# A hybrid encoder block in fp32: another order of first loads, zero products in front, and sums of squares moved from VectorE to GpSimd

## The chip, the cores and the metric

The kernel runs on one core of a Trainium2 chip. The metric is device time in microseconds (us) of one execution. TensorE is called PE, its weight loads PEld, VectorE DVE, ScalarE ACT, GpSimd POOL, and SyncE, whose queue issues nearly all loads, SP.

## The reference, cut to what matters

One layer over 512 tokens of width 2048, all in float32:

```
xn = rmsnorm(x, norm_mix)            # mean of squares over the 2048 channels
y  = xn @ W_in                       # 2048 x 7552, split in two groups of heads
h  = x + concat[GDN(y), RWKV7(y)] @ W_out
h += CrossAttn(rmsnorm(h), rmsnorm(mem))
h += square(relu(rmsnorm(h) @ W_up)) @ W_down
out = rmsnorm(h)
```

The change touches only the beginning: `rmsnorm(x)` and the first products of `xn @ W_in`.

## The kernel before, in words

Channels lie on the 128 partitions and tokens along the free dimension, so `x` is 16 tiles of 128x512 (k = 0 to 15). Every float32 operand of the big products is split into a high part in the PE's faster format (fp32r) and the rest: `hi = cast(v)`, `lo = v - hi`. A product is then three matmuls, hi·hi, hi·lo and lo·hi. For `x` the channel gain `norm_mix` is put in at the split (`xin`): ACT writes `xhi`, DVE writes `xlo` by one scalar_tensor_tensor. The token's factor `rstd` of the rmsnorm is the same for all channels, so it is multiplied in when a finished column tile of `y` is taken out of PSUM (`evict`), and the products can start before it is known.

`projections` runs the 59 column tiles of `W_in`. The first two (n = 0, 1) run side by side, six matmuls for each k, so that few x tiles feed many matmuls; from n = 2 on a tile has 16 x 3 matmuls of its own. Weights come in pieces of 128x1024 (eight k): `loader` loads a piece into `wraw` (three buffers), ACT casts it to `whi`, DVE subtracts to `wlo`. The very first two pieces are cut in halves so that PE can start on 512 columns: `pieceload` loads the first half into a tile `sg`, `pieces` splits it, `rawload` brings the other half. The third and fourth piece (second half of k, n = 0 and 1) go to tiles named `wBK` (hi), `wAR` (lo) and `wGA` (hi), `wGB` (lo).

The x tiles lie in sixteen buffers that are free at the start, and the profile calls them by these names: k = 0 `gq`, 1 `gk`, 2 `gv`, 3 `gz`, 4 `gkn`, 5 `gqn`, 6 `gEs`, 7 `gEG`, 8 `gqd`, 9 `gAq`, 10 `gkt`, 11 `tA`, 12 `E` (or `E2`), 13 `k`, 14 `kp`, 15 `Kt`. `xsum` makes the sum of squares: ACT squares a tile into `sr` (two buffers, in turn) and it is added to an accumulator whose name is `r`. One matmul with ones (`pss`) sums over partitions, and ACT makes `rstd` of it by a logarithm and an exponential. All parameters (`prm`, 262 columns) come in one load.

Up to the end of the attention's key products (some 1050 us), the order on every engine is made by a planner inside the program: each chain (`xin`, `xsum`, `pieces`, `loader`, `projections`, a chain for each head, ...) yields its next operation; `run` takes the one whose inputs are ready first by a cost table (`cost`) and its rank, and `issue` puts it on its engine's queue. Its cost table has a fixed price for each kind of operation, and nothing for one engine holding up another. The engines then work through these queues strictly in order, waiting by semaphores. Behind that stage the order is written out by hand.

The lines that decide the part in question:

```
xr[k] = tl(("gq", "gk", "gv", "gz", "gkn", ...)[k])     # load of x tile k
yield from split_(xr[k], hi, lo, col("norm_mix", k))    # xin: ACT, then DVE
sq = short()                                            # xsum: one of two sr buffers
yield AC.activation(sq, xr[k], AF.Square)
yield DV.tensor_tensor(out=acc, in0=acc, in1=sq, op=ALU.add)
```

Of the kernel before, what the change touches and what calls it, by code (L numbers as in the profile page):

```python
# [9 lines left out]
F32 = mybir.dt.float32  # L10
F32R = mybir.dt.float32r
AF = mybir.ActivationFunctionType
ALU = mybir.AluOpType
# [4 lines left out]
P = 128  # L18
# [55 lines left out]
def build(tc, I, out):  # L74
    nc = tc.nc
    V, S, GP, PE = nc.vector, nc.scalar, nc.gpsimd, nc.tensor
# [9 lines left out]
    pq = pq_cm.__enter__()  # L86

    prm = pc.tile([P, NPRM], F32, name="prm")
    nc.sync.dma_start(prm, I["prm"])
    NC0 = 256  # L90
    cst0 = pc.tile([P, NC0], F32, name="cst0")
    cst = pq.tile([P, NCST - NC0], F32, name="cst")
# [5 lines left out]
    def col(name, i=0):  # L98
        o, w = PRM[name]
        return prm[:, o + i:o + i + 1]  # L100
# [17 lines left out]
    def psb(nm, tag="mx", bufs=2):  # L118
        return tile_of(ps, [P, 512], F32, tag, nm, bufs)

    def mm(o, l, r, start=True, stop=True, again=False):
        PE.matmul(o, l, r, start=start, stop=stop, skip_group_check=again)  # L122
# [17 lines left out]
    def wraw():  # L140
        wcnt[0] += 1
        return tile_of(pw, [P, 1024], F32, "wraw", f"wraw{wcnt[0]}", NWR)
# [32 lines left out]
    def tile_of(pool, shape, dt, tag, nm, bufs):  # L175
        t = pool.tile(shape, dt, tag=tag, name=nm, bufs=bufs)
        turns[tag] = turns.get(tag, -1) + 1
        slot[t.tensor.name] = (tag, turns[tag] % bufs)
        holder[tag, turns[tag] % bufs] = t.tensor.name
        return t  # L180
# [6 lines left out]
    def where(a):  # L187
        n = a.tensor.name
        k = slot.get(n, n)
        assert holder.get(k, n) == n, (n, holder[k])  # L190
        return (k, part(a)) if k in parted else k
# [16 lines left out]
    DV, AC, GS, TE, SY = (Lane(e, k) for e, k in ((V, "DVE"), (S, "ACT"), (GP, "POOL"), (PE, "PE"), (nc.sync, "SP")))  # L208

    def cost(op):  # L210
        eng, nm, _, a, k, out, ins, _ = op
        n = out.free_size()
        if eng == "PE":
            l = ins[0]
            if l.dtype == F32R:
                return n * 0.417 + (13.3 if state["shape"] is None else 120.0)
            sh = (l.partition_size(), l.free_size())
            sw = 0 if state["shape"] == sh or sh == (128, 128) else 100
            if nm == "transpose":
                return sw + (110 if sh[0] > 64 else 40)  # L220
            if sh == (64, 64):
                return sw + (32 if op[5].tensor.name[:2] in ("ri", "gi", "pa", "pv", "pu", "pw", "pk", "po", "pp") else 59)
            if sh[0] < 128 and n == 512:
                return sw + 530
            return sw + (115 if sh[0] < 128 and n == 128 else 2 * max(n * 0.84, 114))
        if eng == "DVE":
            if nm == "memset":
                return 60 + 0.3 * n
            if nm == "tensor_scalar":
                return 210 + 0.45 * n  # L230
            if nm == "tensor_tensor_scan":
                return 90 + 2.2 * n
            return 190 + 1.05 * n if nm == "scalar_tensor_tensor" else 154 + 1.05 * n
        if eng == "ACT":
            need = {AF.Tanh: "e", AF.Ln: "l", AF.Exp: "e"}.get(a[2] if len(a) > 2 else None)
            return (140 + 0.885 * n + 80 * sum(isinstance(x, bass.AP) for x in k.values())
                    + (40 if len(a) > 2 else 0) + (1283 if need and need != state["table"] else 0))
        if eng == "POOL":
            return 116 + 0.75 * n if nm == "memset" else 235 + 2.3 * n
        return 100.0  # L240

    def start(op):
        eng, out = op[0], where(op[5])
        t = clock[eng]
        for b, log in [(where(i), landed) for i in op[6]] + [(out, landed), (out, seen)]:
            x, by = log.get(b, (0.0, eng))
            if op[1] == "dma_start" and by == "DMA" and b == out and log is landed:
                continue
            t = max(t, x + op[7][0] + (0.0 if by == eng else CROSS))
        return t  # L250

    def issue(op):
        eng, nm, f, a, k, out, ins, slack = op
        t = start(op)
        d = cost(op)
        f(*a, **k)  # L256
        if nm == "dma_start":
            clock[eng] = t + (60 if eng == "ACT" else 620 if any(x.tensor.name[:2] in ("bg", "nd") for x in [out] + ins) else 330)
            size = math.prod(out.shape) * 4
            state["dma"] = max(state["dma"], t + 330) + size / 300  # L260
            t, eng = max(state["dma"] + 700, t + 2900) + slack[1], "DMA"
        else:
            t += d
            clock[eng] = t
        if eng == "PE":
            state["shape"] = None if ins[0].dtype == F32R else (ins[0].partition_size(), ins[0].free_size())
        if eng == "ACT" and len(a) > 2 and a[2] in (AF.Tanh, AF.Ln, AF.Exp):
            state["table"] = "l" if a[2] == AF.Ln else "e"
        landed[where(out)] = (t, eng)
        for i in ins:  # L270
            b = where(i)
            if seen.get(b, (0.0, 0))[0] < t:
                seen[b] = (t, eng)
# [7 lines left out]
    def after(*ev):  # L281
        return lambda: ev in events
# [45 lines left out]
    def split_(src, hi, lo, gain=None):  # L328
        if gain is None:
            yield AC.copy(hi, src)  # L330
            yield DV.tensor_tensor(out=lo, in0=src, in1=hi.bitcast(F32), op=ALU.subtract)
        else:
            yield AC.activation(hi, src, AF.Copy, scale=gain)
            yield DV.scalar_tensor_tensor(out=lo, in0=src, scalar=gain, in1=hi.bitcast(F32),
                                          op0=ALU.mult, op1=ALU.subtract)
# [20 lines left out]
    rstd = pc.tile([P, T], F32, name="rstd")  # L356
# [6 lines left out]
    def tl(tag, w=512, bufs=1, shape=None):  # L363
        cnt[0] += 1
        return tile_of(pm, shape or [P, w], F32, tag, f"{tag}_{cnt[0]}", bufs)
# [52 lines left out]
    raws, halves, used, whole, piece = {}, {}, set(), set(), {}  # L418

    def pieceload(i):  # L420
        piece[i] = tl("sg", 512, NSH["sg"])
        return SY.dma_start(piece[i], wq[i][1][:, 0:512])

    def rawload(i):
        raws[i] = wraw()
        if i in piece:
            return SY.dma_start(raws[i][:, 512:], wq[i][1][:, 512:])
        o = raws[i] if len(wq[i][1].shape) == 2 else raws[i].rearrange("p (a b) -> p a b", b=M)
        return SY.dma_start(o, wq[i][1])
# [39 lines left out]
    def pieces():  # L469
        for i in piece:  # L470
            halves[i] = hi, lo = wsplit()
            yield from split_(piece[i], hi[:, 0:512], lo[:, 0:512])
            events.add(("piece", i))

    def half(i):
# [3 lines left out]
    xhi, xlo = [], []  # L479
    acc = tl("r")  # L480
    xr = {}
    XA = 8

    def xload(k):
        xr[k] = tl(("gq", "gk", "gv", "gz", "gkn", "gqn", "gEs", "gEG", "gqd", "gAq", "gkt", "tA", "E2", "k", "kp", "Kt")[k])
        return SY.dma_start(xr[k], I["xT"][:, k, :])

    def xin():
        for k in range(KD):
            hi, lo = act_tile(f"xhi{k}"), act_tile(f"xlo{k}")  # L490
            yield from split_(xr[k], hi, lo, col("norm_mix", k))
            xhi.append(hi)
            xlo.append(lo)
            if k + XA < KD:
                yield xload(k + XA)

    def xsum():
        yield AC.activation(rstd[:, 0:1], b_one, AF.Ln)
        for k in range(KD):
            yield lambda: len(xhi) > k  # L500
            if k == 0:
                yield AC.activation(acc, xr[k], AF.Square)
            else:
                sq = short()
                yield AC.activation(sq, xr[k], AF.Square)
                yield DV.tensor_tensor(out=acc, in0=acc, in1=sq, op=ALU.add)
        yield after("consts")
        pt = psb("pss", "scr", 1)
        yield TE.matmul(pt, ones, acc, start=True, stop=True)
        yield from rsq_(rstd, pt, 1.0 / 2048, b_eps6)  # L510
# [742 lines left out]
    def ahead():  # L1253
        yield after("rows")
        for j in range(NSET):
            chain(presums([tl(f"ds{j}{i}", PIECE, shape=[P, PIECE]) for i in range(4)], PIECE, after("kp", 15)),
                  lambda eng: 2 if eng == "SP" else PRANK)

    issue(pieceload(0))
    issue(xload(0))  # L1260
    issue(pieceload(1))
    issue(xload(1))
    issue(rawload(0))
    issue(rawload(1))
    for k in range(2, 6):
        issue(xload(k))
    issue(rawload(2))
    for k in range(6, XA):
# [430 lines left out]
    acc = ph.tile([P, T], F32, tag="acc", name="acc2", bufs=1)  # L1699
    alloc(range(7))  # L1700
    for n in range(KD):
        if n < 2:
            pt = begun[n][0]
            attend(*begun[n], 1)
        else:
            pt = psb(f"at{n}", "mm", 2)
# [712 lines left out]
```

## Time and profile before

| | |
|---|---|
| time before, median of 3 runs | 2906.9 us (2904.82, 2906.92, 2906.9) |
| profiled execution, own time | 2904.46 us |
| its span, first to last instruction | 2902.7 us |
| PE busy | 2870.4 us (99% of the span) |
| DVE, ACT, POOL busy | 2330.4, 1570.0, 223.6 us |
| PE waits for its first operand | 7.8 us |
| granted PE clock, mean | 0.998 |

A row of the timeline gives start, duration, engine, line, operation, output<-inputs and shape; in brackets the idle time of the engine just ahead of it and what ended that. A duration contains start-up and tail that overlap with the next instruction: the distance between the starts of two rows that follow each other is what an instruction costs its engine. L256 is the planner's `issue`, through which most instructions go, so tiles tell them apart. In the program's order, a name may carry the number of its buffer.

### The profile page before, as it was taken

Reading aid. Unit: us, or ns where it says so; the run is one execution under the profiler, and the core shown is the slowest. Engines: PE = TensorE matmul, PEld = TensorE weight load, DVE = VectorE, ACT = ScalarE, POOL = GpSimd, SP = SyncE. Lnnn points to the kernel's source line nnn. Section 1 sums busy time; section 2 is a strip of 40 time slices with the busy share of each in tenths; the row PEclk is TensorE's granted clock in tenths of the full one; section 3 lists DMA queues with packets and bytes.
Section 4 is the critical chain, followed back from the end, with each engine's and each line's share of the span. In section 5 each row is a group of like instructions: output and inputs, shape, how many; then the busy total and the mean of one; then the engine's idle time right before and its main releaser. Section 6 shows DMA issues by size and latency. Waiting matters only on the chain.

```text
span 2902.7 us, 49242 instructions
## 1 busy us (share of the span) xinstructions
PE 2870.4 (99%) x18794; PEld 2420.3 (83%) x18794; DVE 2330.4 (80%) x3547; ACT 1570.0 (54%) x2233; POOL 223.6 (8%) x547
## 2 busy tenths in 40 slices
PE   8999999999999999999999999999999999999998
PEld 7877877787877888889988888888888888888887
DVE  7787787787887877769956898898998878787888
ACT  6454555555655655564445656555555645454544
POOL 0213213213223000000000000000000000000000
PEclk9999999999999999999999999999999999999999
DMA  5646656656666788784423354565566868978733
GB/s 190 175 139 184 164 156 181 160 150 187 176 163 188 219 249 280 227 286 159 127 92 95 106 163 152 193 199 193 186 201 191 283 225 278 295 257 272 270 100 109
DMA packets 319773, 553.02 MB, mean 191 GB/s; under 512 B 100968, under 2 KB 186220, under 8 KB 319536
## 3 DMA queue, kind: packets, MB, share of 16 engines
q1 hardware_dynamic: 292144, 518.41, 58.0%
q10 hardware_dynamic: 27392, 31.46, 3.1%
q8 instruction: 147, 2.41, 0.3%
q14 instruction: 90, 0.74, 0.1%
HBM read 443.45 MB, written 106.31 MB: 189 GB/s over the span
## 4 chain that ended last, share of the span: by engine, by line
PE 93%; DMA 3%; DVE 2%; ACT 1%; issue 1%; POOL 0%; ACTq 0%; SPq 0%; DVEq 0%; POOLq 0%
PE py L256 22%; PE mxu L256 12%; PE mgu L256 6%; PE mgd L256 6%; PE mxd L256 6%; PE op L122 6%; PE vp L122 3%; PE sc L122 3%; PE at L122 3%; PE mmd L256 3%; PE kp L256 3%; PE mmu L256 3%; PE scrd L256 3%; PE scgd L256 3%; PE kq L256 3%; PE vo L122 1%
## 5 line engine op out<-in xcount | busy, mean ns | idle before, releaser
L256 ACT CAST whi<-wraw 128x1024 fp32r<-128x1024 f32 (+1 forms) x366 | 383.7, 1049 | 399.8 <-PE py L256 146.8
L256 DVE TENSOR_TENSOR wlo<-wraw,whi 128x1024 fp32r<-128x1024 f32 (+1 forms) x366 | 450.4, 1231 | 102.7 <-ACT whi L256 92.9
L256 PE MATMUL py<-xhi,whi 128*128 128x512 f32 x928 | 372.2, 401 | 7.8 <-ACT xhi L256 7.8
L256 PE MATMUL py<-xlo,whi 128*128 128x512 f32 x928 | 373.7, 403 | 0.0
L256 PE MATMUL py<-xhi,wlo 128*128 128x512 f32 x928 | 372.9, 402 | 0.0
L256 ACT CAST whi<-w 128x1024 fp32r<-128x1024 f32 x176 | 185.4, 1054 | 203.9 <-PE mxu L256 48.3
L256 DVE TENSOR_TENSOR wlo<-w,whi 128x1024 fp32r<-128x1024 f32 x176 | 214.8, 1221 | 51.5 <-ACT whi L256 49.5
L256 PE MATMUL mxu<-cb,whi 128*128 128x512 f32 x1016 | 255.0, 392 | 0.0
L256 PEld LDWEIGHTS py<-xhi,whi 128*128 128x128 f32 x928 | 175.0, 189 | 42.1 <-ACT xhi L256 7.8
L256 PEld LDWEIGHTS mxu<-cb,whi 128*128 128x128 f32 x1016 | 182.8, 189 | 32.7
L256 PEld LDWEIGHTS py<-xlo,whi 128*128 128x128 f32 x928 | 175.0, 189 | 35.5 <-DVE xlo L256 0.9
L256 PEld LDWEIGHTS py<-xhi,wlo 128*128 128x128 f32 x928 | 175.1, 189 | 35.1 <-issue 1.8
L131 DVE TENSOR_TENSOR wlo<-wraw,whi 128x1024 fp32r<-128x1024 f32 x112 | 136.6, 1221 | 45.5 <-ACT whi L130 42.5
L130 ACT CAST whi<-wraw 128x1024 fp32r<-128x1024 f32 x112 | 117.7, 1051 | 85.5 <-PE op L122 29.1
L256 PEld LDWEIGHTS mxu<-cb,wlo 128*128 128x128 f32 x1016 | 138.7, 190 | 10.5 <-DVE wlo L256 0.7
L256 PE MATMUL mxu<-cb,wlo 128*128 128x256 f32 x1016 | 142.2, 282 | 0.3 <-DVE wlo L256 0.3
L256 ACT ACT_TABLE_LOAD x87 | 111.6, 1283 | 36.4 <-DVE suml_gn L256 15.5
L256 PE MATMUL mgu<-cb,whi 128*128 128x512 f32 x512 | 129.4, 394 | 1.4 <-ACT whi L256 1.3
L256 PE MATMUL mxd<-whi,cb 128*128 128x512 f32 x512 | 126.7, 389 | 0.0
L256 PE MATMUL mgd<-whi,cb 128*128 128x512 f32 x512 | 126.5, 389 | 0.0
L256 ACT CAST whi<-ws 128x1024 fp32r<-128x1024 f32 x75 | 78.9, 1052 | 75.4 <-PE mgu L256 49.2
L122 PE MATMUL op<-ob,whi 128*128 128x256 f32 (+1 forms) x752 | 115.3, 304 | 0.0
(946 smaller groups left out, 6452.3 us busy)
## 6 DMA issues: line engine op xcount, KB each, us to landing
wraw<-in_w_in SPq DMA_DIRECT2D x116, 512.0 KB, 4.5
wraw<-in_w_up SPq DMA_DIRECT2D x65, 512.0 KB, 3.8
w<-in_w_up SPq DMA_DIRECT2D x63, 512.0 KB, 3.9
ds<-in_w_dm SPq DMA_DIRECT2D x128, 205.0 KB, 4.0
sd_s<-ds SPq DMA_DIRECT2D x128, 205.0 KB, 5.2
wraw<-sd_s SPq DMA_DIRECT2D x51, 512.0 KB, 5.1
w<-sd_s SPq DMA_DIRECT2D x50, 512.0 KB, 5.0
w<-in_w_dm SPq DMA_DIRECT2D x48, 512.0 KB, 5.1
```

The lines of the kernel that those rows point to most:

```text
L122: PE.matmul(o, l, r, start=start, stop=stop, skip_group_check=again)
L130: S.copy(hi, src)
L131: V.tensor_tensor(out=lo, in0=src, in1=hi.bitcast(F32), op=ALU.subtract)
L256: f(*a, **k)
```

## The change

1. The first x tile (`gq`) is loaded from ACT's queue, ahead of everything on it; on SP's queue the first weight half comes first.
2. Of the parameters only the 16 columns of `norm_mix` are loaded at the start, into a tile `prm0` that `xin` uses; all 262 columns follow behind the two second weight halves.
3. x tiles 1, 2 and 3 are loaded ahead of the second weight halves.
4. The two first weight halves (`sg`) are cast on DVE, not on ACT, and the second of them only when the first x tile is split.
5. The 15 additions of the sum of squares run on POOL, not on DVE.
6. Fifteen float32 matmuls of a 128x128 block of zeros with itself stand in front on PE (`warm`, outside the planner). They write to a PSUM tile that nobody reads.

```diff
-    nc.sync.dma_start(prm, I["prm"])
+    prm0 = pq.tile([P, 16], F32, name="prm0")
...
     def pieces():
         for i in piece:
             halves[i] = hi, lo = wsplit()
-            yield from split_(piece[i], hi[:, 0:512], lo[:, 0:512])
+            if i:
+                yield lambda: len(xhi) > 0
+            yield DV.tensor_copy(hi[:, 0:512], piece[i])
+            yield DV.tensor_tensor(out=lo[:, 0:512], in0=piece[i], in1=hi[:, 0:512].bitcast(F32), op=ALU.subtract)
             events.add(("piece", i))
...
-    def xload(k):
+    def xload(k, SY=SY):
...
-            yield from split_(xr[k], hi, lo, col("norm_mix", k))
+            yield from split_(xr[k], hi, lo, prm0[:, k:k + 1])
...
-                yield DV.tensor_tensor(out=acc, in0=acc, in1=sq, op=ALU.add)
+                yield GS.tensor_tensor(out=acc, in0=acc, in1=sq, op=ALU.add)
...
+    warm = rstd[:, P:2 * P]
+    V.memset(warm, 0.0)
+    pt = psb("warm", "scr", 1)
+    for _ in range(15):
+        mm(pt[:, 0:P], warm, warm)
+    issue(xload(0, Lane(nc.scalar, "ACT")))
     issue(pieceload(0))
-    issue(xload(0))
+    issue(SY.dma_start(prm0, I["prm"][:, 0:16]))
     issue(pieceload(1))
     issue(xload(1))
+    issue(xload(2))
+    issue(xload(3))
     issue(rawload(0))
     issue(rawload(1))
-    for k in range(2, 6):
+    issue(SY.dma_start(prm, I["prm"]))
+    for k in range(4, 6):
         issue(xload(k))
```

Since the planner's clock now runs otherwise, it also orders other instructions anew. On ACT, the stretch from the cast of the third weight piece (`wBK`) to that of the fourth (`wGA`) stood like this before (`xhi` rows split an x tile, `sr` rows square one):

```order
L256 CAST wBK<-wraw_219 128x1024
L256 ACTIVATE xhi_320<-gEs_221,prm 128x512
L256 ACTIVATE sr_330<-gv_211 128x512
L256 ACTIVATE xhi_347<-gEG_223,prm 128x512
L256 ACTIVATE xhi_358<-gqd_255,prm 128x512
L256 ACTIVATE xhi_369<-gAq_269,prm 128x512
L256 CAST wGA<-wraw_277 128x1024
```

The same stretch of ACT now:

```order
L256 CAST wBK<-wraw_238 128x1024
L256 ACTIVATE xhi_345<-gEs_240,prm_73 128x512
L256 ACTIVATE sr_355<-gkn_234 128x512
L256 ACTIVATE xhi_374<-gEG_242,prm_73 128x512
L256 ACTIVATE xhi_386<-gqd_267,prm_73 128x512
L256 ACTIVATE xhi_397<-gAq_282,prm_73 128x512
L256 ACTIVATE xhi_404<-gkt_292,prm_73 128x512
L256 ACTIVATE xhi_412<-tA_305,prm_73 128x512
L256 ACTIVATE sr_379<-gqn_236 128x512
L256 CAST wGA<-wraw_321 128x1024
```

Three rows more (x tiles 10 and 11 and a square) now stand between `wBK` and `wGA`. On DVE, in the stretch that ends with the low part of the fourth piece (`wGB`), the order was:

```order
L256 SCALAR_TENSOR_TENSOR xlo_311<-gqn_217,prm,xhi_310 128x512
L256 TENSOR_TENSOR r_178<-r_178,sr_279 128x512
L256 TENSOR_TENSOR wAR<-wraw_219,wBK 128x1024
L256 SCALAR_TENSOR_TENSOR xlo_321<-gEs_221,prm,xhi_320 128x512
L256 SCALAR_TENSOR_TENSOR xlo_348<-gEG_223,prm,xhi_347 128x512
L256 SCALAR_TENSOR_TENSOR xlo_359<-gqd_255,prm,xhi_358 128x512
L256 SCALAR_TENSOR_TENSOR xlo_370<-gAq_269,prm,xhi_369 128x512
L256 TENSOR_TENSOR r_178<-r_178,sr_330 128x512
L256 TENSOR_TENSOR wGB<-wraw_277,wGA 128x1024
```

And on DVE now:

```order
L256 TENSOR_TENSOR wAR<-wraw_238,wBK 128x1024
L256 SCALAR_TENSOR_TENSOR xlo_346<-gEs_240,prm_73,xhi_345 128x512
L256 SCALAR_TENSOR_TENSOR xlo_375<-gEG_242,prm_73,xhi_374 128x512
L256 SCALAR_TENSOR_TENSOR xlo_387<-gqd_267,prm_73,xhi_386 128x512
L256 SCALAR_TENSOR_TENSOR xlo_398<-gAq_282,prm_73,xhi_397 128x512
L256 SCALAR_TENSOR_TENSOR xlo_405<-gkt_292,prm_73,xhi_404 128x512
L256 SCALAR_TENSOR_TENSOR xlo_413<-tA_305,prm_73,xhi_412 128x512
L256 TENSOR_TENSOR wGB<-wraw_321,wGA 128x1024
```

The sums (`r_178`, the accumulator) are gone from DVE, and `wGB` stands two x tiles later. On POOL the sums are now in front of and behind three memsets:

```order
L256 TENSOR_TENSOR r_178<-r_178,sr_379 128x512
L256 TENSOR_TENSOR r_178<-r_178,sr_421 128x512
L256 MEMSET WTz 128x896
L256 MEMSET BTz 128x896
L256 MEMSET TtG 128x512
L256 TENSOR_TENSOR r_178<-r_178,sr_442 128x512
L256 TENSOR_TENSOR r_178<-r_178,sr_482 128x512
```

Six sums stand ahead of the memsets (the last two of them are shown) and nine behind. On PE, `pss` stands 16 rows earlier in the sequence of `py` matmuls (129 of them stand ahead of it). From the inversion of the fifth RWKV head (`ri4`) to the end of the planned stage, PE's order is that of before.

## The prediction

> **What bounds the kernel now.** I read the page first, then PE's waits, then the timeline of the first 25 us.
>
> ```profile
> span 2902.7 us, 49242 instructions
> PE 2870.4 (99%) x18794; PEld 2420.3 (83%) x18794; DVE 2330.4 (80%) x3547; ACT 1570.0 (54%) x2233; POOL 223.6 (8%) x547
> PE py L256 <- ACT xhi L256: 7.8, 1, 7.8
> PE kp L256 <- ACT whi L256: 2.4, 1, 2.4
> PE pkk L256 <- DVE gk L256: 2.2, 1, 2.2
> PE ri7u L256 <- DVE k L256: 2.0, 1, 2.0
> ```
>
> PE is busy 99% of the span, so nearly every microsecond by which its stream of matmuls is put off or brought forward at the start is still there at the end. Its longest wait is the first: 7.8 us until the first x tile is split. The next three lie where PE's order is that of before, so I leave them as they are.
>
> The timeline shows what the first 7.8 us are made of (SPq rows are issues of loads):
>
> ```profile
> 0.75 0.40 SPq L89 DMA_DIRECT2D prm<-in_prm  x1
> 1.21 0.42 SPq L256 DMA_DIRECT2D sg<-in_w_in  x1
> 1.67 0.43 SPq L256 DMA_DIRECT2D gq<-in_xT  x1
> 4.92 0.62 ACT L256 CAST whi<-sg 128x512 fp32r<-128x512 f32 x1 [2.68 <-DMA sg<-in_w_in]
> 7.04 0.72 ACT L256 ACTIVATE xhi<-gq,prm 128x512 fp32r<-128x512 f32 x1 [1.50 <-DMA gq<-in_xT]
> 7.82 0.79 PE L256 MATMUL py<-xhi,whi 128*128 128x512 f32 x1 [7.82 <-ACT xhi L256]
> ...
> 11.33 0.60 PE L256 MATMUL py<-xlo,whi 128*128 128x512 f32 x1
> 11.76 0.41 PE L256 MATMUL py<-xhi,wlo 128*128 128x512 f32 x1
> ...
> 15.66 0.39 PE L256 MATMUL py<-xhi,whi 128*128 128x512 f32 x1
> 15.88 0.39 PE L256 MATMUL py<-xlo,whi 128*128 128x512 f32 x1
> ```
>
> Three loads stand in a row (131, 256 and 256 KB); ACT starts at each landing. Matmuls start 0.43 us apart up to 11.76 and 0.22 to 0.23 apart later: PE runs at half its clock for its first 3.9 us. The row at 15.66 is the first matmul on x tile 4 (`gkn`).
>
> **The change part by part: what it gains.** The first matmul needs `gq`, the weight half and `norm_mix`. Before, 387 KB (prm and sg) had landed at 4.92 and 643 KB at 7.04. Now sg, gq and 8 KB of parameters are 520 KB: in proportion 6.0 us. With the ACT split (0.72) and the hand-over that the rows show (7.04 to 7.82) `xhi` reaches PE at 6.8. The zero products must be through by then as well. Float32 products of 128 columns are in the trace, at full clock:
>
> ```profile
> 200.40 0.60 PE L256 MATMUL gpo<-gAq,gE 128*128 128x128 f32 x4
> ...
> 201.88 0.48 PE L256 MATMUL py<-xlo,whi 128*128 128x512 f32 x1
> ```
>
> Between these two rows stand 14 passes of `gpo` (two a product): 0.106 us a pass. Fifteen products are 30 passes, 3.2 us at full and 6.4 us at half clock. They begin behind DVE's memset, about 1.2 us, so they end between 4.4 and 7.6; if the clock rises 3.9 us after their start, as it did after 7.82, it rises at 5.1 and they end at 6.4. The first real product comes at about 7.0 (6.8 to 7.6), and at full clock: its eight slow matmuls up to 11.76 took 3.9 us and would take 8 x 0.23 = 1.8. Casting `sg` on DVE costs between 0.42 (tensor_scalar of 128x512, next row) and 0.69 us (tensor_tensor, below); I take 0.45, and it lies in DVE's wait for the first x tile.
>
> ```profile
> 57.13 0.42 DVE L256 TENSOR_SCALAR gAq<-gAq 128x512 f32<-128x512 f32 x1
> 5.30 0.63 SPq L256 DMA_DIRECT2D gkn<-in_xT  x1
> gkn<-in_xT SPq DMA_DIRECT2D x1, 256.0 KB, 7.5
> ```
>
> So PE may run up to 2.9 us ahead, but loads cap it. Ahead of `gkn` the queue holds the same bytes as before and 8 KB more. It was issued at 5.30 and landed 7.5 us later, at 12.8; split and handed over it reaches PE at 13.6, against 15.66 before. At the fifth tile PE is ahead by 2.1 us at most.
>
> **What it gives back: the order of ACT and DVE.** The fourth weight piece (`wGA`, `wGB`) is needed for the 54th matmul. These rows show that need and the costs on the way:
>
> ```profile
> 22.27 0.39 PE L256 MATMUL py<-xhi,wGB 128*128 128x512 f32 x1
> ...
> 18.34 0.71 ACT L256 ACTIVATE xhi<-gAq,prm 128x512 fp32r<-128x512 f32 x1
> 18.98 1.06 ACT L256 CAST wGA<-wraw 128x1024 fp32r<-128x1024 f32 x1
> 19.94 0.72 ACT L256 ACTIVATE xhi<-gkt,prm 128x512 fp32r<-128x512 f32 x1
> 20.56 0.62 ACT L256 ACTIVATE sr<-gz 128x512 f32<-128x512 f32 x1
> 21.08 0.71 ACT L256 ACTIVATE xhi<-tA,prm 128x512 fp32r<-128x512 f32 x1
> ...
> 16.09 1.23 DVE L256 TENSOR_TENSOR wAR<-wraw,wBK 128x1024 fp32r<-128x1024 f32 x1
> 17.23 0.75 DVE L256 SCALAR_TENSOR_TENSOR xlo<-gEs,prm,xhi 128x512 fp32r<-128x512 f32 x1
> 17.89 0.75 DVE L256 SCALAR_TENSOR_TENSOR xlo<-gEG,prm,xhi 128x512 fp32r<-128x512 f32 x1
> ```
>
> By the distances of starts an x tile costs ACT 0.62, a 1024 cast 0.96, a square or a 512 cast 0.52; DVE pays 1.14 for a 1024 difference and 0.66 for an x tile. On ACT, from the split of `gkn` (12.8) to the cast `wGA`, there now stand eight x tiles (5.0), one 512 cast and three squares (2.1) and `wBK` (1.0): 8.1 us, so `wGA` starts at 20.9 and ends at 21.9. The difference `wGB` (1.2) is then ready at 23.1 if DVE does nothing else. Before, PE had it at 22.27 without waiting. So a lead of 2.1 us turns into a delay of 0.8 here, even without POOL.
>
> **What POOL adds.** Fifteen sums of 0.69 us leave DVE and go to POOL. An add of this size on POOL, and what happens beside it, are in the trace:
>
> ```profile
> L256 DVE TENSOR_TENSOR r<-r,sr x15: 681/692/693, 15.5 to 42.3; 128x512 f32<-128x512 f32 x15
> 119.50 1.29 POOL L256 TENSOR_TENSOR gEs<-gE,cst 128x512 f32<-128x512 f32 x1
> 120.13 1.75 DVE L256 TENSOR_TENSOR wlo<-wraw,whi 128x1024 fp32r<-128x1024 f32 x1 [0.17 <-ACT whi L256]
> ...
> 346.40 1.36 DVE L256 TENSOR_TENSOR wlo<-wraw,whi 128x1024 fp32r<-128x1024 f32 x1 [1.39 <-ACT whi L256]
> 346.97 1.94 POOL L256 TENSOR_TENSOR gEs<-gE,cst 128x512 f32<-128x512 f32 x1 [0.30 <-ACT gE L256]
> ```
>
> POOL needs 1.29 us. The DVE difference that began 0.63 us into it took 1.75 instead of 1.23: it stood until POOL was done. At 346.97 it was the other way round: POOL took 1.94, the excess of 0.65 being what the difference that ended at 347.76 still had to run. So these two exclude each other, less some 0.15 us at the edge. [...]
>
> In the stretch that decides, DVE works through eight x tiles (5.3), a 512 difference (0.6), two small parameter rows (0.2), `wAR` (1.1) and `wGB` (1.2), 8.4 us from 13.6: it would be through at 22.0, inside the 23.1 above. Three of POOL's sums (the squares in ACT's stretch) fall among them, each holding DVE for 1.29 - 0.15 = 1.14 us: 3.4 us more, so `wGB` is ready at 25.4 rather than 23.1. PE waits twice on the way, about 2.5 us for `xlo` of `gEs` (behind `wAR` and a sum) and 2.5 us for `wGB`, and its 54th matmul starts at 25.4 instead of 22.27: **+3.1 us**. With edges of 0.05 or 0.25 us and one sum more or less in the stretch it is +1.7 to +3.8; without any exclusion +0.8.
>
> Next comes `pss`, which PE takes in order; behind it stand the matmuls of n = 2 and 3. It needs all 15 sums. After the 54th matmul 76 stand ahead of it: 25.4 + 76 x 0.23 = 42.9. POOL has ten sums (12.9) and three memsets (0.84 + 0.84 + 0.52 in the trace's rows, 2.1 by starts) from about 23.2: 38.2 bare. Seven DVE instructions come between (four `xlo`, three `wlo`), holding POOL for up to 0.5 or 1.0 us each, 5.0 at most; I take 3. The sums are done at 41 to 43: `pss` just about does not wait. **0**.
>
> **The clock gate.** Does PE lose its full clock in those two waits? Three stretches of 3.41 us, the width of the one in which the trace has a lower clock (busy PE, PEld, DVE, ACT, POOL, then PEclk):
>
> ```profile
> 916.30:919.71 3.41, 2.45 (x43) 1.92 (x42) 0.91 (x3) 1.46 (x4) 0.00 (x0) 1.00 1.00 363
> 929.95:933.37 3.42, 1.44 (x65) 1.20 (x64) 2.92 (x6) 1.75 (x3) 2.15 (x5) 1.00 0.32 92
> 933.37:936.78 3.41, 3.41 (x16) 2.65 (x9) 3.26 (x5) 1.41 (x4) 3.01 (x6) 0.50 0.56 175
> ```
>
> With PE busy 1.44 of 3.42 us (the 2.0 us wait for `ri7u`) the next stretch ran at 0.50; with 2.45 it stayed full. In such a stretch about 8 matmuls pass instead of 15, 1.7 us lost. A wait of 2.5 us leaves too little in one stretch if most of it falls into one, which depends on where the stretches lie: I take one chance in two for the second wait (a loss behind the first is swallowed by the second): **+0.9**. [...]
>
> **The sum.** +3.1 + 0 + 0.9 = +4.0 us, on the profiled execution's 2904.46 (1.8 us more than its span) 2908.5. The median of the runs is 2906.9, 2.4 above the profiled one; on it the forecast is **2910.9**. A measurement of this kernel can tell about 0.2%, 5.8 us, from no change: the forecast lies within that. The rest of PE's order hardly changes its mix, and its waits up to the fifth head are small, for which I allow 1 us either way.
>
> **The rivals.** *Slower than the bound:* the sums end late. If each of the seven DVE instructions holds POOL for its whole length (4 x 0.66 + 3 x 1.14 = 6.1), the sums end at 44.3 and `pss` holds PE 1.4 us; with the clock halved after `wGB`, 3.1 + 1.4 + 1.7 = +6.2, and with +3.8 at `wGB` +6.9: 2913.1 to 2913.8. It decides from the point where the last sum ends after 42.9. For it: exclusion is plain in both pairs of rows. Against: the edges overlap, and a halved clock gives POOL time. 33%.
>
> *The exclusion hardly bites:* sums fall into gaps of DVE, and only ACT's order counts: +0.8, 2907.7. For it: the difference at 346.40 ran before POOL and lost little (0.13). 11%.
>
> *Faster than the bound:* the lead of 2.1 us stays (the fourth piece lands and is cast in time), the halved clock at 933 is not met (1.7), and of the three late waits (6.6 together) about a third goes: -6.0, 2900.9. Against: those waits stand behind an unchanged order, and ACT alone puts `wGA` at 20.9. 6%.
>
> *The zero products do not do what they are for:* they end at 7.6, or the clock falls again in the short waits for the first `xlo`. That costs up to 2.1 us before the fifth tile and nothing behind it, since the wait for `wGB` swallows it; it is inside the forecast.
>
> **How the numbers follow.** Forecast 50%, the two others within the bound or over it as given: same 0.50 + 0.11 = 0.61, slower 0.33, faster 0.06. The range leaves out the faster rival and the far end of the slow one: 2904.5 (hardly any exclusion, 0.8, on the lower of the runs, 2904.82, and 1 us of luck) to 2915.0 (slow rival and 1 us).
>
> **What would show it.** First real matmul near 7.0 and starts 0.23 apart; `xhi` of `gkn` near 12.8; PE's row on `wGB` near 25.4, behind a wait on DVE `wlo` or `xlo` of 2 to 3 us; POOL's sums and DVE's two-input rows stretched in turn; `pss` near 43. Wrong is the forecast if `wGB` is there by 23, or if PE is held at `pss` by more than 2 us.

## The result, and the profile after

The changed kernel takes 2913.2 us (median of 7 runs, 2911.28 to 2917.1), the kernel before in runs on the same chip 2903.5 (7 runs, 2902.16 to 2906.92): a ratio of 1.0032, 95% interval 1.002 to 1.0043. That is 9.7 us more by the medians, over the bound of 0.2%. The predicted time of 2910.9 us lay too low, the range (to 2915.0) holds the median, and the outcome lies on the side of the slow rival.

The profiled execution took 2911.63 us (before 2904.46). Its page and its list of PE's waits (us in total, times, longest):

```profile
span 2909.8 us, 49302 instructions
PE 2878.7 (99%) x18824; PEld 2427.2 (83%) x18824; DVE 2338.9 (80%) x3543; ACT 1569.7 (54%) x2231; POOL 248.5 (9%) x562
PE py L256 <- DVE xlo L256: 2.7, 3, 1.4
PE py L256 <- DVE wGB L256: 2.6, 1, 2.6
PE kp L256 <- ACT whi L256: 1.7, 1, 1.7
PE ri7u L256 <- DVE k L256: 1.4, 1, 1.4
```

The span is 7.1 us longer. The first wait of 7.8 us is gone; 5.3 us for `xlo` and `wGB` stand in its place, and the late waits for `kp` and `ri7u` are 1.3 us shorter than before. The beginning on PE, from its timeline:

```profile
1.18 5.67 PE L122 MATMUL warm<-rstd 128*128 128x128 f32 x30 [1.18 <-DVE rstd L1263]
6.60 0.48 PE L256 MATMUL py<-xhi,whi 128*128 128x512 f32 x1
12.55 0.39 PE L256 MATMUL py<-xhi,whi 128*128 128x512 f32 x1
25.49 0.51 PE L256 MATMUL py<-xhi,wGB 128*128 128x512 f32 x1 [2.59 <-DVE wGB L256]
44.56 1.02 PE L256 MATMUL pss<-r,cst 128*128 128x512 f32 x2
```

At x tile 4 (12.55) PE is 3.1 us ahead of before (15.66); at the 54th matmul (25.49) it is 3.2 behind (22.27). In between, ACT, DVE and POOL:

```profile
11.14 0.72 ACT L256 ACTIVATE xhi<-gkn,prm 128x512 fp32r<-128x512 f32 x1 [0.54 <-DMA gkn<-in_xT]
19.09 1.03 ACT L256 CAST wGA<-wraw 128x1024 fp32r<-128x1024 f32 x1
20.65 0.62 ACT L256 ACTIVATE sr<-gEs 128x512 f32<-128x512 f32 x1
...
14.08 1.79 DVE L256 SCALAR_TENSOR_TENSOR xlo<-gqn,prm,xhi 128x512 fp32r<-128x512 f32 x1
15.79 1.31 DVE L256 TENSOR_SCALAR prm<-prm 128x1 f32<-128x1 f32 x2
19.49 1.78 DVE L256 SCALAR_TENSOR_TENSOR xlo<-gqd,prm,xhi 128x512 fp32r<-128x512 f32 x1
21.86 1.78 DVE L256 SCALAR_TENSOR_TENSOR xlo<-gkt,prm,xhi 128x512 fp32r<-128x512 f32 x1
24.22 1.21 DVE L256 TENSOR_TENSOR wGB<-wraw,wGA 128x1024 fp32r<-128x1024 f32 x1
...
13.66 1.66 POOL L256 TENSOR_TENSOR r<-r,sr 128x512 f32<-128x512 f32 x1 [1.62 <-ACT sr L256]
15.74 1.30 POOL L256 TENSOR_TENSOR r<-r,sr 128x512 f32<-128x512 f32 x1 [0.42 <-ACT sr L256]
19.32 1.40 POOL L256 TENSOR_TENSOR r<-r,sr 128x512 f32<-128x512 f32 x1 [2.28 <-ACT sr L256]
21.41 1.68 POOL L256 TENSOR_TENSOR r<-r,sr 128x512 f32<-128x512 f32 x1 [0.69 <-ACT sr L256]
25.09 15.56 POOL L256 TENSOR_TENSOR r<-r,sr 128x512 f32<-128x512 f32 x9
```

`wGA` is cast by 20.1, but the difference `wGB` only starts at 24.22, because four DVE rows behind 13.6 took about 1.04 us more than they do alone (an `xlo` 0.74; the two parameter rows at 15.79, merged into one line, 0.27 in e9 below): each waited for a sum of POOL's. The parameter rows have a single input of 128x1. POOL's last nine sums took 1.73 us each, in turn with DVE's rows, and were done at 40.65, ahead of `pss` at 44.56. Behind the wait PE's granted clock falls to 0.50 (the columns are those of the prediction's stretches):

```profile
22.59:26.00 3.41, 0.82 (x4) 0.46 (x3) 3.41 (x4) 2.50 (x4) 3.41 (x5) 1.00 0.70 281
26.00:29.41 3.41, 3.41 (x9) 2.65 (x9) 3.41 (x3) 2.19 (x3) 3.25 (x3) 0.50 0.86 207
```

### The profile page after: what moved, and what is told of

Its sections match the earlier page's. It is cut to its first block, busy times and chain, and to the rows that moved or that the text cites. A ratio compares the mean times of both kernels' runs of the same rounds, so it can differ in the third digit from the quotient of the medians.

```text
span 2909.8 us, 49302 instructions
## 1 busy us (share of the span) xinstructions
PE 2878.7 (99%) x18824; PEld 2427.2 (83%) x18824; DVE 2338.9 (80%) x3543; ACT 1569.7 (54%) x2231; POOL 248.5 (9%) x562
## 4 chain that ended last, share of the span: by engine, by line
PE 91%; DMA 3%; DVE 2%; ACT 1%; issue 1%; POOL 0%; ACTq 0%; SPq 0%; DVEq 0%; POOLq 0%
PE py L256 21%; PE mxu L256 12%; PE mgd L256 6%; PE mxd L256 6%; PE mgu L256 6%; PE op L122 5%; PE vp L122 3%; PE sc L122 3%; PE at L122 3%; PE mmd L256 3%; PE mmu L256 3%; PE kp L256 3%; PE scrd L256 3%; PE scgd L256 3%; PE kq L256 3%
```

## The experiments

Times are medians, the ratio is to the kernel before in runs on the same chip; "wGB" is the start of the 54th matmul. Span, wGB and the stretches at half clock (their starts up to 1140 us) are those of the one profiled execution; a number in brackets tells how many stretches follow each other.

| kernel | time, us | ratio, 95% | span | wGB | half clock at |
|---|---|---|---|---|---|
| before | 2903.5 to 2904.7 | 1 | 2902.7 | 22.27 | 933 |
| after | 2913.2 | 1.0032 [1.002, 1.0043] | 2909.8 | 25.49 | 26, 924 |
| e1 memsets for sums | 2907.3 | 1.0011 [1.0002, 1.0019] | 2905.0 | 21.96 | 920 |
| e2 sums on DVE, order of after | 2909.3 | 1.0014 [1.0005, 1.0023] | 2909.6 | 22.99 | 920, 1131 |
| e9 first six sums on DVE | 2908.3 | 1.0018 [1.0009, 1.0026] | 2909.6 | 22.50 | 226, 922, 1134 |
| e10 sums of half width | 2908.2 | 1.0014 [1.0005, 1.0023] | 2907.7 | 22.54 | 922 |
| e3 before, sums on POOL | 2910.7 | 1.0021 [1.0012, 1.003] | 2910.1 | 23.31 | 38 |
| e5 after without part 5 | 2906.4 | 1.0002 [0.9993, 1.001] | 2907.8 | 21.87 | 935 |
| e4 before and zeros | 2905.2 | 1.0001 [0.9992, 1.001] | 2903.0 | | 933 |
| e6 after, one zero product | 2914.3 | 1.0036 [1.0024, 1.0048] | 2912.5 | 25.84 | 26, 924 |
| e7 before, early loads | 2910.5 | 1.0023 [1.0014, 1.0032] | 2904.6 | | 926 |
| e11 before, early loads, zeros | 2903.8 | 1.0001 [0.9992, 1.001] | 2901.3 | | none |
| e8 another plan | 2910.4 | 1.0023 [1.0015, 1.0031] | 2912.9 | | 225, 501, 692, 928 |
| e12 a second other plan | 2930.8 | 1.0095 [1.0081, 1.0109] | 2931.2 | | 593 (2), 835 (3), 849 (2), 859 (2) |

Theory: GpSimd's sums hold DVE, DVE is late with `wGB`, and the wait there halves the clock. Rivals: the new order, the new loads or the zeros cost the time.

**e1, the sums replaced by memsets of POOL** (1.47 us for a sum's 1.30, in the same places of the same order; the sums are left out):

```diff
-yield GS.tensor_tensor(out=acc, in0=acc, in1=sq, op=ALU.add)
+o = GS.tensor_tensor(out=acc, in0=acc, in1=sq, op=ALU.add)
+def fill(out, in0, in1, op):
+    for c in (512, 512, 240):
+        GP.memset(in1[:, 0:c], 0.0)
+yield o[:2] + (fill,) + o[3:]
```

> The changed kernel with every engine's order kept; each of the 15 sums on POOL is replaced by three memsets of the same sr buffer (together about 1.3 us), so POOL still makes ACT wait in the same way but reads no SBUF. The sums themselves are left out. Exclusion theory: no DVE row is stretched any more (x-tile rows 0.75, not 1.78), wGB is ready at about 21.3 (wGA ends at 20.1, plus 1.2) and PE uses it 4 us earlier than at 25.49, without a wait over 1.5 us and without the halved clock at 26.0: span 4 to 6 us shorter than the changed kernel's 2909.8, so 2904 to 2906. Rival 'order alone' (ACT and DVE reach wGB late whatever POOL does): wGB stays near 25, span within 1 us of 2909.8. Rival 'later order' (the loss is made behind 50 us): wGB early, but span still above 2908.

DVE, POOL and PE in its timeline:

```profile
18.80 0.74 DVE L256 SCALAR_TENSOR_TENSOR xlo<-gkt,prm,xhi 128x512 fp32r<-128x512 f32 x1
19.47 0.74 DVE L256 SCALAR_TENSOR_TENSOR xlo<-tA,prm,xhi 128x512 fp32r<-128x512 f32 x1
20.68 1.22 DVE L256 TENSOR_TENSOR wGB<-wraw,wGA 128x1024 fp32r<-128x1024 f32 x1 [0.47 <-ACT wGA L256]
...
19.77 1.47 POOL L513 MEMSET sr<- 128x512 f32 x3 [2.12 <-ACT sr L256]
...
21.96 0.50 PE L256 MATMUL py<-xhi,wGB 128*128 128x512 f32 x1 [0.53 <-DVE wGB L256]
39.40 1.02 PE L256 MATMUL pss<-r,cst 128*128 128x512 f32 x2
```

POOL is as busy as in the changed kernel, but no `xlo` is held, `wGB` starts 3.54 us earlier and the clock stays full. PE is 3.5 us ahead of the changed kernel at the 54th matmul and 5.2 at `pss` (39.40 against 44.56), with the same matmuls between: the 1.6 more is the halved stretch, near the 1.7 that the prediction gives it. At the end 4.8 are left. That is the theory's part, shown. (In e1's execution x tile 4 came to ACT 0.5 us later, at 11.66, so 3.5 is rather too little.) Left is +2.3 us of span against before, 1.0011 in the times: the order, the loads and the zeros together.

**e2, the sums on DVE in the order of after** (`o[:2] + (V.tensor_tensor,) + o[3:]` for the sum, all orders kept), and **e9, only the first six of them** (`(V if k < 7 else GP).tensor_tensor`):

> The changed kernel with the planner still told that the sums run on POOL, so PE, ACT and SP keep their order row for row, but the sums are executed by DVE at their planned places. Exclusion theory: three sums of 0.6 us stand ahead of wGB instead of three blocks of 1.0, no block: wGB used by PE at 22 to 23.5, no halved clock at 26, the span 3.5 to 5 us shorter than 2909.8 (2905 to 2906.5). Rival 'order alone': wGB near 25 and span near 2910, since DVE now has even more to do.

> The changed kernel in the changed kernel's order, with the first six of the fifteen sums (those ahead of wGB) executed by VectorE in the places where GpSimd did them; the nine behind stay on GpSimd. Theory (only the sums ahead of wGB cost time): wGB's first matmul at 22.7 to 23.4 us as with all sums on VectorE in this order (22.99), no half clock before 900 us, VectorE's rows behind 25 us still 1.7 us long, and the time 2908 to 2911 us. Rival (the nine behind cost as much): 2912 us or more.

In e2 the 54th matmul waits 1.71 us and the clock stays full behind the stretch in which most of that wait lies:

```profile
22.99 0.50 PE L256 MATMUL py<-xhi,wGB 128*128 128x512 f32 x1 [1.71 <-DVE wGB L256]
...
21.88:25.29 3.41, 2.30 (x10) 1.92 (x11) 3.41 (x5) 3.41 (x6) 0.00 (x0) 1.00 1.11 395
```

The time is 1.0014 of before. The front came out as expected, the span did not: 2909.6 us, the rival's figure, where 2905 to 2906.5 were expected. At `pss` (40.44) PE is 4.1 us ahead of the changed kernel, so the span was lost later: this execution lies near the top of e2's times and waited 2.1 us for `vp`, with half a clock behind it at 1131 (the changed kernel has none there). e9's DVE and PE rows, and its stretches around 226 us:

```profile
26.00 1.79 DVE L256 SCALAR_TENSOR_TENSOR xlo<-Kt,prm,xhi 128x512 fp32r<-128x512 f32 x1
...
22.50 0.50 PE L256 MATMUL py<-xhi,wGB 128*128 128x512 f32 x1 [1.68 <-DVE wGB L256]
...
222.57:225.98 3.41, 1.27 (x36) 0.75 (x36) 1.59 (x6) 1.65 (x4) 2.71 (x10) 1.00 0.58 209
225.98:229.39 3.41, 3.41 (x40) 2.93 (x33) 2.13 (x4) 1.32 (x4) 2.88 (x9) 0.50 0.32 90
```

Behind `wGB` DVE is held as before (1.79), and yet the time is that of e2 within the intervals: what is measurable of the cost comes from the sums ahead of `wGB`. The 54th matmul came 0.2 us earlier than expected, and "no half clock before 900" was missed: a wait of 1.9 us for `BK` halved it at 226.

**e10, sums over 256 of the 512 columns:**

```diff
+GP.tensor_tensor(out=out[:, 0:256], in0=in0[:, 0:256], in1=in1[:, 0:256], op=op)
```

> The changed kernel, each of GpSimd's sums done on 256 of its 512 columns (the sum over the other columns is left out); every order as it was. Theory (VectorE is held for as long as a row of GpSimd's runs): the row alone takes 0.6 to 0.8 us, a 128x512 split on VectorE that meets one takes 1.3 to 1.5 us instead of 1.78, wGB's first matmul comes at 23.2 to 24.3 us, and with a wait there under 2 us the clock is not halved before 900 us: 2908 to 2911 us. Rival (a meeting has a fixed price): VectorE's rows stay at 1.7 us, wGB at 25 us or later, 2912 us or more.

```profile
20.13 1.22 DVE L256 SCALAR_TENSOR_TENSOR xlo<-tA,prm,xhi 128x512 fp32r<-128x512 f32 x1
...
20.03 0.77 POOL L512 TENSOR_TENSOR r<-r,sr 128x256 f32<-128x256 f32 x1 [2.36 <-ACT sr L256]
```

A held `xlo` takes 1.22, not 1.78: the hold is 0.48 for a sum of 0.77 us, and 1.04 for one of 1.30. So here it went with the length of the other engine's row, 0.26 to 0.29 us less than that, and had no fixed price (1.3 to 1.5 us were expected for the `xlo`). `wGB` came at 22.54, earlier than the 23.2 expected, as fewer rows met a sum: between 13.6 us and `wGB` three were held and not four.

**e3, the order of before with the sums on POOL:**

> The kernel before with its own order on PE, ACT and SP kept row for row; only the 15 sums are executed by POOL. Exclusion theory: two sums fall ahead of wGB, each a block of about 1.0 for a relief of 0.6: wGB ready at 21.7 to 22.3, so hardly a wait there; later the 13 other sums alternate with DVE and end at 43 to 46 where pss stands at 43.4: +0 to +2.5 us on before. Rival 'POOL is only relief for DVE': equal or faster by up to 1 us.

```profile
PE py L256 <- DVE wlo L256: 2.9, 1, 2.9
PE pss L256 <- POOL r L256: 1.7, 1, 1.7
...
45.26 5.82 POOL L256 TENSOR_TENSOR r<-r,sr 128x512 f32<-128x512 f32 x4 [7.36 <-ACT sr L256]
```

The expectation was missed by far: 1.0021. In the old order many squares come late, behind weight casts. Eight sums alternate with `xlo` rows, casts and weight differences, and four more come only from 45.26 on. PE waits 2.9 us for a `wlo`, the clock is halved at 37.7, and `pss`, at 51.1 instead of 43.4, is held 1.7 us. That is the mechanism of the prediction's slow rival, in another kernel than the one it was made for.

**e5, part 5 undone in the source** (`DV.tensor_tensor` again, planned anew; the other five parts stay):

> The changed kernel with part 5 undone in its source: VectorE adds the squares again, and the planner makes its own order for that; the other five parts stay. Theory (GpSimd's sums hold VectorE up, and that is most of the loss): no 128x512 row of VectorE ahead of 25 us takes over 0.8 us, wGB's first matmul starts between 21.5 and 23.5 us instead of 25.49, the clock stays full until 900 us, and the time is 2903 to 2909 us, the width being what another order behind the front can do (plus or minus 3 us). Rival (the other loads and the casts on VectorE cost the time): wGB at 24 us or later, and 2910 us or more.

`wGB` at 21.87 behind a wait of 0.52, no clock lost there, and a ratio of 1.0002 [0.9993, 1.001]. The five other parts together cost nothing that can be measured. PE's order up to `ri4` is here that of before, but for the place of `pss`. All of the loss hangs on the move of the sums: by holding DVE, and by the order that the planner made for it. (The profiled execution, with its span of 2907.8, is the slowest of the eleven.)

**e4, e6, e7 and e11: what the front is worth.** e4 puts the zero products in front of the kernel before; e6 leaves one of fifteen (`range(1)`) in the changed one; e7 makes the loads early in the order of before; e11 has both, and loads all parameters at once behind the first x tile (in part; the remarks are not in the code):

```diff
-    nc.sync.dma_start(prm, I["prm"])
+    nc.sync.dma_start(prm0, I["prm"][:, 0:16])       # xin uses prm0
...
+    issue(o[:2] + (nc.scalar.dma_start,) + o[3:])    # x tile 0, from ACT's queue
+    nc.scalar.dma_start(prm, I["prm"])               # e11; in e7 on SP's, behind rawload(1)
```

> The kernel before with only the 15 zero products put in front (order otherwise kept). My reading: matmuls from 7.8 on start 0.23 apart, but x tile 2 reaches PE only at 12.2 instead of 12.7, so at most 0.5 us is won: the same time within 1 us. Rival 'the clock is worth its whole 2 us': 2 us faster. Rival 'zeros delay the start' (end after 7.8): slower by up to 0.5 us.

> The changed kernel with one product of zeros in front instead of fifteen, all else and every order as it was. Theory (PE's later waits for x tiles and for wGB take the front's lead anyway): the clock is half until 10 to 12 us, the first real matmul stays at 6.6 us, but wGB's first matmul stays within 0.4 us of 25.49, since DVE's rows set it, and the time stays within 1.5 us of 2913.2. Rival (the zeros pay in this order): about nine matmuls at half clock cost 0.2 us each, wGB's first matmul and the end come 1.5 to 2 us later, 2914.7 us or more.

> The kernel before with every order of its engines' arithmetic kept; only the loads change: the first x tile from ScalarE's queue, sixteen columns of parameters first, all 262 behind the second weight halves. Theory (a lead at the front is taken back by later waits in the stage of the heads): the first matmul starts at 6.4 to 7.0 us instead of 7.82, the lead at the first sum of squares is 0.5 to 1.5 us, a third of it or less is left at 590 us, and the time is 2902 to 2905 us, no change that can be measured. Rival (a lead at the front is kept): 2902 us or less, with the lead at 590 us as it was at 43 us.

> The kernel before with its arithmetic in its own order, the first x tile from ScalarE's queue with all parameters right behind it there, sixteen columns of them first on SyncE's, and fifteen products of zeros in front. Theory (a lead at the front is real, and shrinks in the heads' stage): the first real matmul starts at 6.4 to 7.1 us and takes 0.23 us, the lead at the 13th matmul is 1.2 to 2.5 us, at 590 us 0.3 to 1.5 us, and the time is 2901.5 to 2904.5 us. Rival (VectorE's row on all parameters holds its queue up again, as with the early loads alone): PE waits over 1 us for the first xlo, and 2906 us or more.

The times of e4 and e6 came out as expected: the matmuls at half clock (up to 11.76 in before, up to 12.13 in e6) cost nothing that can be measured at the end in either order. The first real matmul did not: at 6.06 in e6 rather than 6.6, at 6.70 in e4 rather than 7.8. In e4 PE is up to 2.6 us ahead at the ninth matmul and then waits for x tile 2:

```profile
11.04 0.51 PE L256 MATMUL py<-xhi,whi 128*128 128x512 f32 x1 [0.79 <-ACT xhi L256]
```

Following the same matmuls through both traces, the lead is 1.2 us from 16 to 200 us, 0.5 at 230, 0.2 at 500 us and gone at 790. Not even the 1.2 is the zeros' own: x tiles 0 and 2 reached ACT at 5.93 and 10.27 in this execution, at 7.04 and 11.46 in that of before. In e3, with the same loads and no zeros, tile 0 came at 5.96: single executions differ by 1.1 us here. e7 was missed, for a reason that I had overlooked:

```profile
8.77 0.18 DVE L257 TENSOR_SCALAR dp<-prm 128x27 f32<-128x27 f32 x1 [7.25 <-DMA prm<-in_prm]
...
11.14 0.80 PE L257 MATMUL py<-xlo,whi 128*128 128x512 f32 x1 [3.83 <-DVE xlo L257]
```

In the old order the first rows of DVE's queue read all parameters; the late load held everything behind them, and PE waited 3.8 us for its second matmul. (In the order of after `dp` stands behind two x tiles.) This delay of 2.5 us was still 2.9 at 814 us; unlike a lead, it is not taken back in the heads' stage, but at 1127 us 0.9 of it is left. The profiled execution (2906.4) is the fastest of ten; why the median lies 4 us above it stays open. e11 mends that wait: a lead of 1.0 us at the 13th matmul (1.2 to 2.5 were expected), none at 590 us, and 2903.8 us, no different from before. Of the variants run, this is the best, and it does not beat before.

**e8 and e12, another order and nothing else.** The planner's landing time of a load is set to 2600 and to 3200 ns, where it was 2900:

```diff
-t, eng = max(state["dma"] + 700, t + 2900) + slack[1], "DMA"
+t, eng = max(state["dma"] + 700, t + 2600) + slack[1], "DMA"
```

> The kernel before with one number of its planner changed: it takes a load to land 2600 ns after its issue, where it took 2900. The same instructions, in another order. Theory (a new order by itself moves the end by some us): the first ri4u matmul is 1.5 us or more away from 585.7 us on either side and the time 1 to 5 us away from the kernel before. Rival (the order behind the front is neutral): ri4u within 1 us of 585.7, time within 1 us.

> The kernel before with its planner's landing time of a load set to 3200 ns, where it was 2900: the same instructions in a second other order. Theory (the order of before is better than most, and another one costs 1 to 6 us): ri4u 1 us or more from 585.7 us, time 2906 to 2911 us. Rival (the first other order, at 2910.4 us, was an unlucky one, and orders lie on both sides): 2904.5 us or less.

PE's waits from 60 to 900 us, in before and in e12:

```profile
PE gn L256 <- DVE suml_gn L256: 1.6, 3, 0.8
PE rs L256 <- DVE Qs L256: 1.1, 1, 1.1
```

```profile
PE ri6s L256 <- DVE k L256: 4.5, 1, 4.5
PE rs L256 <- DVE BK L256: 3.5, 3, 2.7
PE ri4s L256 <- DVE k L256: 3.1, 1, 3.1
```

The same instructions in another order cost 0.23% and 0.95%. Waits in the heads, which the order of before keeps at 2.7 us in all, come back (10 us in e8, 4 of them for DVE; 20 in e12, 19 of them for DVE), and some of the longer ones halve the clock besides: e8 has three such stretches between 60 and 900 us and e12 nine, before none. (e8's ri4u was at 586.3, within 1 us of before; its delay came later, +5.7 at ri6u.) All three other orders of PE that were run, these two and that of the changed kernel, lose against that of before. Three are few, but they speak for an order near the good end.

## Why the prediction was right or wrong

- **The front.** First matmul at 6.60 (predicted 7.0), 0.23 us apart, and 3.1 us ahead at tile 4 (2.1 at most predicted). The proportion of bytes was too slow for the loads: `gkn` was landed by 11.1, not 12.8. Part of the 3.1 is chance: with the loads of before, the first matmul started at 7.8 in three traces and at 6.7 in two (e3, e4). That a microsecond won at the start is still there at the end was wrong for such leads (e4, e11), and right for what was lost at `wGB`: 5.2 us between e1 and the changed kernel at `pss`, 4.8 at the end.
- **ACT's order.** Its eight x tiles and the rest took 7.95 us (11.14 to 19.09) where 8.1 were counted. But they began 1.7 us earlier, so `wGA` was cast by 20.1 instead of 21.9, and without POOL the 54th matmul comes at 21.96 (e1), not 23.1: -0.3 in place of +0.8.
- **POOL.** The mechanism was right; the term was too small. Four sums fall in the stretch, not three, each holding DVE 1.04 us (predicted 1.14): 4.2 us, of which e1's DVE, waiting for ACT, had 0.8 to spare. Measured +3.5 (25.49 - 21.96) for +2.3. That 25.49 came so near 25.4 is luck: this error and that of ACT's order cancel. The count was low because I took the three squares ahead of `wGA` on ACT. The fourth sum is that of `gEs`, squared right behind `wGA` (20.65): DVE, held three times by then, was still ahead of `wGB` when it came. And one of the three met rows of one input (1.31 us for the two, 0.27 in e9), which I had not expected to be held. Of the two waits of 2.5 us only that for `wGB` came (2.59); `xlo` of `gEs` cost 1.38, two others 0.7 each. `dp`, also of one input, took 1.27 us here against 0.18 in before, and beside e1's memsets on POOL the two-input `xlo` rows stayed at 0.74.
- **`pss`.** Right: asked for at 44.56, done at 40.65. The slow rival's mechanism did not happen here; its sign was right for another reason.
- **The clock.** A chance of one half, +0.9; it happened, +1.7. PE was busy 0.82 of the 3.41 us ahead of it. In the fourteen traces, cut from the first change of the clock into stretches of 3.41 us, each one with at most 1.48 us of busy PE was followed by a halved one and none with 1.79 or more; in between (1.54 to 1.77) five were and seven not. So in these traces it went with whether PE was busy for about half of a stretch, and with it with how a wait lay over the stretches: the wait of 2.2 us for `pkk` halved the clock in the changed kernel, e1, e2, e6, e9 and e10, and not in before, e3, e4, e5, e7 and e11. The length alone does not tell: single waits of 1.9 us (e9, at 226) to 2.9 us (e3, at 38) halved it, and one of 2.4 us (before, `kp` at 921) did not.
- **"The rest of PE's order hardly changes its mix … 1 us either way."** This is the step that failed. In e1, with nothing else of the loss in it (loads and zeros cost nothing in e11), the span is +2.3 us; e2, e9 and e10, which keep this order too and have no halved stretch at `wGB`, are 1.0014 to 1.0018 of before. The mix itself costs: ahead of the first `ri4u` stand the same 4896 matmuls in both orders, and PE, at full clock, is busy 578.5 us with them in the new order (e1; 578.4 in e2, 578.1 in e10), 575.8 in that of before (e4; 575.7 in e11, 576.0 in e5). The lines of e1 and e4, from the first matmul to `ri4u` (length, PE busy, rows, clock, DMA share, GB/s):

```profile
6.49:588.93 582.44, 578.47 (x4900) 1.00 0.60 171
6.70:585.44 578.74, 575.84 (x4896) 1.00 0.60 170
```

That is 2.5 us without a wait that shows (the ends of PE's rows are modelled, so very short waits may hide in it); which neighbours cost it is not taken apart. Besides, PE's waits between 60 and 900 us grow from 2.7 to 4.9 us, with 2.9 for `pak` on `BK` that before did not have; the waits for `kp` and `ri7u`, which I left as they were, shrink from 4.4 to 2.0 and give as much back. Added up, with the 0.3 us by which e1 is ahead at the 54th matmul, -0.3 + 2.5 + 2.2 - 2.4 = 2.0, near the 2.3. And it is not even-sided: e8 and e12 lost 6 and 27 us by order alone.

With what was measured the sum is -0.3 + 3.5 + 1.7 = 4.9 at the front, and 2.6 by what e1 leaves (its +2.3 and the 0.3 us that it was ahead): 7.5, against 7.1 in the span. The medians differ by 9.7 us, the interval is 5.8 to 12.5 us; the rest is not traced to a place. That the range holds the time is in part luck: the forecast added 4.0 us to a median of 2906.9 from three runs, and in seven runs the kernel before has 2903.5. So the change was 5.7 us more than forecast, and the time only 2.3.

## What to carry to other kernels

Before work is moved to GpSimd, lay its rows over VectorE's queue and ask which reader waits for the row behind each meeting: here a sum of 1.3 us cost VectorE 1.0 to 1.1, whether it met an `xlo` (1.78 for 0.74) or a small parameter row (`dp`, 1.27 for 0.18), and only those ahead of a row that PE waits for cost time that could be measured (e9). A lead in front of a fixed order was worth little where later waits took it back (e4's 1.2 us was gone at 790), while a delay could stay (that of e3 did, 7.9 us at 60 us and 7.5 at the end; that of e7 shrank to a third behind the heads). And where a planner makes the order, count the new order as a likely cost, also in busy time that no wait shows: undo the edit in its execution but keep its order (as e1 and e2 do) to see what the order alone does.

## What was not expected of the hardware

A DVE cast with one input took longer among memsets of POOL, where two-input rows did not: `onesr` took 0.22 us before, 0.97 among e1's memsets (e1's `xlo` rows 0.74), and 1.32 among the changed kernel's sums. Behind the start, half-clock stretches in these traces were 3.41 us long or a multiple of it (6.83 and 10.24 us in e12). Near 930 us before has one, behind a wait of 2.0 us for `ri7u`; e11, with 1.4 us there, has none.
